# A ReGLU MLP on one core: weight-block sums moved from an engine to accumulating DMAs, with a DMA-turned second half of x, wider output homes and an exit hint

## The chip, the cores and the metric

One core of one Trainium2 chip. The metric is device time in microseconds (us) of one execution; every time below is a median over the runs named. The record sorts executions into fast and slow by their time and the clock granted to TensorE. Engine names in the profile: PE is TensorE's matmul stream, PEld its weight loads, DVE is VectorE, ACT ScalarE, POOL GpSimd, SP SyncE. SPq and POOLq are the issuing sides of those engines.

## The reference

```python
x:  (16, 256, 512)   w1: (512, 4096)   w2: (2048, 512)      # float32
h = x @ w1
gate, value = np.split(h, 2, axis=-1)
h = np.maximum(gate, 0) * value
return (h @ w2).astype(np.float32)
```

## The kernel before

The 4096 rows of x are handled in four *sets* of 1024. Both matmuls are done in float16 by a recursive scheme with seven products of half-size blocks in place of eight. It needs sums of blocks of the weights (T1 to T4) and of the moving operand (S1 to S4):

```python
TURNS = (("T1", "B12", "B11", SUB), ("T2", "B22", "T1", SUB), ("T3", "B22", "B12", SUB), ("T4", "B21", "T2", SUB))
SUMS  = (("S1", "A21", "A22", ADD), ("S2", "S1", "A11", SUB), ("S4", "A12", "S2", SUB), ("S3", "A11", "A21", SUB))
WX = {"P1": ("B11", "A11"), "P2": ("B21", "A12"), "P3": ("B22", "S4"), "P4": ("T4", "A22"),
      "P5": ("T1", "S1"), "P6": ("T2", "S2"), "P7": ("T3", "S3")}
```

The first matmul has 16 *blocks* of hidden columns a set (the first four of the first set are plain products). Its weight sums are the tile `wt`, made chunk by chunk on GpSimd (`w1_ops`). The gated result `g` is the moving side of the second matmul, with its own sums `g_S`. The second matmul's weight sums `v_T` are made once, in the first set, also on GpSimd. In program order, with cuts marked:

```python
if s == 0:
    w1_ops(nc.gpsimd, 4, 2); ...                  # wt of blocks 4-9, loads of w2 between
    for c in range(1, NS):
        cast_x(c)                                 # DRAM to DRAM, f32 to f16, sets 1 to 3, GpSimd's DMA queue
    w1_ops(nc.gpsimd, 10, 2)                      # wt of blocks 10, 11
    w1_ops(nc.gpsimd, 12, 4)                      # wt of blocks 12 to 15
    for m in ("T1", "T2", "T3"):
        w2_op(nc.gpsimd, m)                       # v_T: one 128x2048 tensor_tensor each
for at in ...:                                    # the blocks; products of the last set's second matmul between
    if n == "P1" and s == 0 and jb in (10, 12, 14):
        g_sum(nc.gpsimd, go, "S3", jb - 10, jb - 8)
    ...
if s == 0:
    g_sum(nc.gpsimd, go, "S3", 6, 8)
    w2_op(nc.gpsimd, "T4")
    for m in ("S1", "S2", "S4"):                  # on DVE, two halves each
        for h in (0, NHC // 2):
            g_sum(nc.vector, go, m, h, h + NHC // 2)
```

I call *seam* the stretch from the first product of a set's second matmul to the first block of the next set. In it TensorE has only the second matmul to do, and waits for T and S sums if they are late.

Of the kernel before, what the change touches and what calls it, by code (L numbers as in the profile page):

```python
# [16 lines left out]
P = 128  # L17
TH = 512
PERIOD = 7
NWARM = 7  # L20
NFILL = 4
# [8 lines left out]
@with_exitstack  # L30
def kernel(ctx: ExitStack, tc: tile.TileContext, x, w1, w2, out):






    nc = tc.nc
    x2 = x.flatten_outer_dims()
    out2 = out.flatten_outer_dims()  # L40
    flagpool = ctx.enter_context(tc.tile_pool(name="flagpool", bufs=1))
    flag = flagpool.tile([1, 1], dt.int32, name="flag")
    with ExitStack() as fast:
        unfit = fast_way(fast, tc, x2, w1, w2, out2, flag)
    with tc.If(unfit > 0, preferred_fallthrough_block=False):
        with ExitStack() as general:
            general_way(general, tc, x2, w1, w2, out2)
# [52 lines left out]
def fast_way(ctx, tc, x2, w1, w2, out2, flag):  # L100
# [32 lines left out]
    x16 = {s: dpool.tile([SET, D], F16, name=f"x16_{s}") for s in range(1, NS)}  # L133
# [17 lines left out]
    TURNS = (("T1", "B12", "B11", SUB), ("T2", "B22", "T1", SUB), ("T3", "B22", "B12", SUB), ("T4", "B21", "T2", SUB))  # L151
# [8 lines left out]
    def w2_op(eng, name, n=1):  # L160
        for m, a, b, o in TURNS:
            if m == name:
                for h in range(0, NHC, NHC // n):
                    hs = slice(h, h + NHC // n)
                    eng.tensor_tensor(V[m][:, hs], V[a][:, hs], V[b][:, hs], op=o)

# [3 lines left out]
    ident = {t: wpool.tile([P, P], t, name=f"ident{k}") for k, t in enumerate((F32, F16))}  # L170
# [15 lines left out]
    SUMS = (("S1", "A21", "A22", ADD), ("S2", "S1", "A11", SUB), ("S4", "A12", "S2", SUB), ("S3", "A11", "A21", SUB))  # L186
# [9 lines left out]
    class Block:  # L196
# [25 lines left out]
        def P6(self):  # L222
            self.mm("P6", self.Y, False)
            nc.scalar.activation(self.u2, self.Y, COPY, scale=GS)  # L224
# [9 lines left out]
        def P7(self):  # L234
            self.mm("P7", self.Y, False)
            nc.vector.scalar_tensor_tensor(out=self.c22, in0=self.Y, scalar=GS, in1=self.p5, op0=MULT, op1=ADD)  # L236
# [41 lines left out]
    def mm2_stream(s, go):  # L278
# [14 lines left out]
        def step(name, b):  # L293
# [6 lines left out]
            elif name == "P5":  # L300
                d["W"] = take(psw, "W")
                yield from mm("P5", b, d["W"], True)
                d["pu"] = tmp.tile([P, 2, TH], F32, name="pv", tag="tmp")[:, :, :HALF]
# [5 lines left out]
            elif name == "P6":  # L309
                yield from mm("P6", b, d["Y"], False)  # L310
                nc.scalar.activation(d["pu"][:, 1], d["Y"], COPY, scale=1 / GS)
            elif name == "P3":
                yield from mm("P3", b, d["W"], False)
                nc.vector.scalar_tensor_tensor(out=d["o1"][:, HALF:], in0=d["W"], scalar=1 / GS, in1=d["pu"][:, 1],  # L314
                                               op0=MULT, op1=ADD)
                nc.sync.dma_start(out=out_v[s, 0, b], in_=d["o1"])
            elif name == "P7":
                yield from mm("P7", b, d["Y"], False)
                d["o2"] = tmp.tile([P, DO], F32, name="o", tag="o", bufs=4)
                nc.vector.scalar_tensor_tensor(out=d["o2"][:, HALF:], in0=d["Y"], scalar=1 / GS, in1=d["pu"][:, 0],  # L320
                                               op0=MULT, op1=ADD)
                if last and b == NB - 1:
                    nc.sync.dma_start(out=out_v[s, 1, b, :, HALF:], in_=d["o2"][:, HALF:])
            else:
                yield from mm("P4", b, d["Y"], False)
                if last and b == NB - 1:
                    m = HALF // 2
                    nc.scalar.activation(d["o2"][:, :m], d["Y"][:, :m], COPY, scale=1 / GS)  # L328
                    nc.scalar.dma_start(out=out_v[s, 1, b, :, :m], in_=d["o2"][:, :m])
                    o3 = tmp.tile([P, DO], F32, name="o", tag="o", bufs=4)[:, :m]  # L330
                    nc.vector.tensor_scalar(out=o3, in0=d["Y"][:, m:], scalar1=1 / GS, scalar2=None, op0=MULT)  # L331
                    nc.sync.dma_start(out=out_v[s, 1, b, :, m:HALF], in_=o3)
                else:
                    nc.scalar.activation(d["o2"][:, :HALF], d["Y"], COPY, scale=1 / GS)
                    nc.sync.dma_start(out=out_v[s, 1, b], in_=d["o2"])
# [35 lines left out]
    xh = go["S2"][:, :NB]  # L371
    wl = g[:, NJ - 4:].rearrange("p a t -> p (a t)").bitcast(F32).rearrange("p (e g j) -> p e g j", e=4, g=2)

    def turn_pair(o, b0):
        for b in (b0, b0 + 1):
            ps = psw.tile([P, 4, P], F32, name="W", tag="W")
            for e in range(4):
                nc.tensor.transpose(ps[:, e], xf[:, b, e * P:(e + 1) * P], ident[F32])
# [3 lines left out]
    def turn_half(o, b0, copy):  # L382
        ps = psx.tile([P, 4, 2, P], F16, name="X", tag="X")
        for b in range(2):
            for e in range(4):
                nc.tensor.transpose(ps[:, e, b], xh[:, b0 + b, e * P:(e + 1) * P], ident[F16])
        copy(out=o["A2"][:, :, b0 * P:(b0 + 2) * P], in_=ps.rearrange("p e b t -> p e (b t)"))
# [6 lines left out]

    def look_x(s, i):
        b = i // 2
        t = rows[s, b // 2][:, b % 2] if s else (xf, xh)[b // NB][:, b % NB]
# [6 lines left out]
    fetch_w1(1, 0)  # L404
    make_identity(nc, ident[F32])
    fetch_w1(1, 1)
    nc.gpsimd.dma_start(out=xh[:, :2], in_=x_v[0, :, NB:NB + 2])
    make_identity(nc, ident[F16])
    nc.gpsimd.dma_start(out=xh[:, 2:], in_=x_v[0, :, NB + 2:])
    for c in range(2, len(CHUNKS)):  # L410
# [3 lines left out]
    xo = x_tiles()  # L414
    plain = [Plain(g, jb) for jb in range(NPLAIN)]
# [17 lines left out]
    for p in plain[2:]:  # L433
# [5 lines left out]
        if p is plain[2]:  # L439
            turn_half(xo, 0, nc.vector.tensor_copy)  # L440
    turn_half(xo, 2, nc.scalar.copy)
# [6 lines left out]
    for p in plain:  # L448
        p.open_x()
        p.open_w()  # L450
        if p is plain[0]:
            for q in range(2):
                p.mm(0, xo["A2"], q)
                p.mm(1, xo["A2"], q)
        else:
            p.mm(0, xo["A2"], 0, 2)
            p.mm(1, xo["A2"], 0, 2)
# [11 lines left out]

    def fetch_rows(s, q):  # L470
        rows[s, q] = xpool.tile([P, 2, D], F16, name=f"xn{q % 2}")
        nc.sync.dma_start(out=rows[s, q], in_=x16[s][q * 256:(q + 1) * 256].rearrange("(b p) d -> p b d", p=P))
# [31 lines left out]
    verdict = []  # L504
    BESIDE[NS - 1, 18] = [lambda: verdict.append(nc.values_load(
# [5 lines left out]
    for s in range(NS):  # L511
# [7 lines left out]
        if s == 0:  # L519
# [9 lines left out]
            w1_ops(nc.gpsimd, 10, 2)  # L529
            w1_ops(nc.gpsimd, 12, 4)  # L530
            for m in ("T1", "T2", "T3"):
                w2_op(nc.gpsimd, m)
        for at in range(first * PERIOD, last + PERIOD):
            if at in plan:
# [3 lines left out]
                if n == "P1" and s == 0 and jb in (10, 12, 14):  # L538
                    g_sum(nc.gpsimd, go, "S3", jb - 10, jb - 8)
# [14 lines left out]
        if s == 0:  # L554
            g_sum(nc.gpsimd, go, "S3", 6, 8)
            w2_op(nc.gpsimd, "T4")
            for m in ("S1", "S2", "S4"):
# [6 lines left out]
        if s + 1 < NS:  # L564
            xo = x_tiles()
            for h in range(2):
                for k in range(2):
                    nc.sync.dma_start_transpose(out=xo[f"A{h + 1}{k + 1}"],
                                                in_=x16[s + 1][h * TH:(h + 1) * TH, k * 256:k * 256 + 256])
# [42 lines left out]
```

## Time and profile before

The kernel takes 326.84 us (three runs, 326.08 to 327.3); the profiled execution spans 325.6 us. From the profile's first two parts (busy time and its share of the span; then busy tenths in 40 slices of 8.1 us, and the granted TensorE clock in tenths):

```profile
PE 306.3 (94%) x1868; PEld 183.7 (56%) x1868; DVE 216.9 (67%) x331; ACT 189.0 (58%) x450; POOL 160.3 (49%) x133
...
PE   7999999954999999999999999999999999999892
...
PEclk9999999995999999999999999999999999999998
```

TensorE is the bottleneck, with one visible hole in mid-kernel (the digits 5 and 4), in which the clock also falls to half. The waits of PE name it (line waited at, what released it: total us, times, longest):

```profile
PE Y L285 <- DVE g_S L274: 6.0, 2, 4.4
PE W L285 <- DVE g_S L274: 1.7, 1, 1.7
PE Y L285 <- DVE flag L488: 1.5, 1, 1.5
```

7.7 us are waits for `g_S` sums on DVE, all in the first set's seam; 1.5 us wait for the flag that decides the exit. A further 0.7 us, further down the same list, is for an output tile. Why DVE is late shows in the timelines of the two engines (start us, busy us, engine, line, operation, output<-inputs, count). GpSimd:

```profile
47.52 2.13 POOL L158 TENSOR_TENSOR wt<-wr,wt 128x1024 f16<-128x1024 f16 x1
49.59 4.08 POOL L165 TENSOR_TENSOR v_T<-w_sb 128x2048 f16<-128x2048 f16 x1
53.76 4.07 POOL L165 TENSOR_TENSOR v_T<-w_sb,v_T 128x2048 f16<-128x2048 f16 x1
57.79 4.07 POOL L165 TENSOR_TENSOR v_T<-w_sb 128x2048 f16<-128x2048 f16 x1
61.81 10.32 POOL L274 TENSOR_TENSOR g_S<-g 128x1024 f16<-128x1024 f16 x4
72.10 5.03 POOL L165 TENSOR_TENSOR v_T<-w_sb,v_T 128x2048 f16<-128x2048 f16 x1
```

and DVE:

```profile
65.62 4.53 DVE L274 TENSOR_TENSOR g_S<-g 128x2048 f16<-128x2048 f16 x2
70.08 8.13 DVE L274 TENSOR_TENSOR g_S<-g_S,g 128x2048 f16<-128x2048 f16 x2
78.13 2.35 DVE L274 TENSOR_TENSOR g_S<-g,g_S 128x2048 f16<-128x2048 f16 x2
```

T1 to T3 push S3 to 61.8 and T4 to 72.1, so GpSimd runs beside DVE's sums until 77.1. Each of these DVE lines is a pair of sums: a pair takes 4.5 and 8.1 us beside GpSimd and 2.35 us without it. The Trainium skill, "SBUF — State Buffer", section "Who interferes with whom", says that a DVE instruction with two SBUF inputs contends with a GpSimd instruction that reads SBUF, and that one of the two then waits for the whole of the other; this trace agrees: from the second on, each DVE sum beside GpSimd ends 1.1 us after the GpSimd sum that it met (70.16 after 69.07, 73.22 after 72.14, 78.21 after 77.12).

### The profile page before, as it was taken

To read this page: it belongs to the slowest core of one execution; us is meant where nothing else is said; L and a number is where in the kernel's file an instruction comes from. 1 tells how busy PE (TensorE), PEld (TensorE's weight loads), DVE (VectorE), ACT (ScalarE), POOL (GpSimd) and SP (SyncE) were. 2 spreads that over 40 slices of the span, in tenths; PEclk is the share of its full clock that TensorE was granted. 3 is DMA by queue.
4 is the path that set the end of the run, shared out by engine and by line. 5 is a ranking of instruction groups with operands and counts; after the bars stand their busy time and mean duration, and the time that the engine had idled before them with its cause. 6 is when DMAs were issued, how large, how long until landed. Compare 5 with 4: busy or idle time off the path is not lost. (4 is left out here: it accounts for less than half of the span.)

```text
span 325.6 us, 5158 instructions
## 1 busy us (share of the span) xinstructions
PE 306.3 (94%) x1868; PEld 183.7 (56%) x1868; DVE 216.9 (67%) x331; ACT 189.0 (58%) x450; POOL 160.3 (49%) x133
## 2 busy tenths in 40 slices
PE   7999999954999999999999999999999999999892
PEld 3754444543884444458884444448884444448681
DVE  1377888898736888885525888886525888886210
ACT  3347666532756766755757666665757666663120
POOL 8499999994001334994001344995001344995000
PEclk9999999995999999999999999999999999999998
DMA  7999995260321100026311100018411100000222
GB/s 242 209 203 207 237 204 123 64 131 0 129 81 50 35 32 0 0 44 153 132 64 66 32 30 4 0 31 140 155 67 64 32 31 4 0 2 0 99 85 84
DMA packets 30542, 26.60 MB, mean 82 GB/s; under 512 B 13776, under 2 KB 25936, under 8 KB 30416
## 3 DMA queue, kind: packets, MB, share of 16 engines
q0 software_dynamic: 8080, 9.44, 16.8%
q1 hardware_dynamic: 21232, 15.67, 16.3%
q10 hardware_dynamic: 1200, 1.11, 1.1%
q8 instruction: 16, 0.26, 0.3%
q14 instruction: 14, 0.11, 0.1%
HBM read 24.12 MB, written 11.53 MB: 109 GB/s over the span
## 5 line engine op out<-in xcount | busy, mean ns | idle before, releaser
L274 POOL TENSOR_TENSOR g_S<-g 128x512 f16<-128x512 f16 (+1 forms) x46 | 58.8, 1281 | 127.0 <-DVE g L240 125.1
L203 PEld LDWEIGHTS <-wt 128*128 128x128 f16 x480 | 46.8, 97 | 56.2 <-issue 2.5
L203 PE MATMUL X<-x_A,wr 128*128 128x512 f16 x240 | 71.3, 378 | 0.2 <-ACT Y L210 0.2
L203 PE MATMUL Y<-x_S,wt 128*128 128x512 f16 x240 | 71.4, 379 | 0.0
L230 DVE SCALAR_TENSOR_TENSOR cc<-W,pu 128x512 f32<-128x512 f32 x60 | 41.5, 692 | 35.1 <-ACT pu L224 35.1
L285 PEld LDWEIGHTS <-g_S 128*128 128x128 f16 x512 | 50.5, 99 | 15.0 <-DVE g_S L274 8.5
L203 PEld LDWEIGHTS <-wr 128*128 128x128 f16 x360 | 35.0, 97 | 41.2 <-issue 0.5
L210 ACT COPY Y<-X 128x512 f32<-128x512 f32 x60 | 34.2, 570 | 38.6 <-PE X L203 19.8
L224 ACT ACTIVATE pu<-Y 128x512 f32<-128x512 f32 x60 | 35.8, 597 | 14.4 <-PE Y L203 14.4
L285 PEld LDWEIGHTS <-g 128*128 128x128 f16 x384 | 37.5, 98 | 10.9 <-issue 2.7
L231 DVE SCALAR_TENSOR_TENSOR g<-X,cc 128x512 f16<-128x512 f32 x60 | 41.5, 691 | 2.3
L240 DVE SCALAR_TENSOR_TENSOR g<-Y,cc 128x512 f16<-128x512 f32 x60 | 40.9, 681 | 2.8 <-PE Y L203 2.8
L236 DVE SCALAR_TENSOR_TENSOR cc<-Y,pu 128x512 f32<-128x512 f32 x60 | 40.9, 681 | 0.1
L285 PE MATMUL Y<-v_T,g_S 128*128 128x256 f16 x256 | 32.0, 279 | 6.0 <-DVE g_S L274 6.0
L217 ACT ACTIVATE pu<-W 128x512 f32<-128x512 f32 x60 | 36.2, 603 | 0.0
L203 PE MATMUL W<-x_S,wt 128*128 128x512 f16 x120 | 35.7, 379 | 0.0
L203 PE MATMUL W<-x_S,wr 128*128 128x512 f16 x120 | 35.7, 379 | 0.0
L203 PE MATMUL Y<-x_A,wt 128*128 128x512 f16 x120 | 35.5, 377 | 0.0
L285 PE MATMUL X<-w_sb,g 128*128 128x256 f16 x256 | 31.2, 273 | 0.0
L314 DVE SCALAR_TENSOR_TENSOR o<-W,pv 128x256 f32<-128x256 f32 x16 | 6.8, 425 | 34.3 <-PE W L285 25.0
L274 POOL TENSOR_TENSOR g_S<-g,g_S 128x512 f16<-128x512 f16 x18 | 21.8, 1213 | 1.4
L274 POOL TENSOR_TENSOR g_S<-g_S,g 128x512 f16<-128x512 f16 x18 | 20.8, 1155 | 1.4
(69 smaller groups left out, 315.3 us busy)
## 6 DMA issues: line engine op xcount, KB each, us to landing
out_dram<-o SPq DMA_DIRECT2D x31, 256.0 KB, 2.0
x<-in_x_dram POOLq DMA_DIRECT2D x3, 1024.0 KB, 15.1
xn<-x SPq DMA_DIRECT2D x12, 256.0 KB, 2.9
wr<-in_w_dram POOLq DMA_DIRECT2D x4, 512.0 KB, 14.4
w_sb<-in_w_dram POOLq DMA_DIRECT2D x4, 512.0 KB, 11.3
wr<-in_w_dram POOLq DMA_DIRECT2D x6, 256.0 KB, 10.3
g<-in_w_dram ACTq DMA_DIRECT2D x2, 512.0 KB, 7.1
g_S<-in_x_dram SPq DMA_DIRECT2D x2, 512.0 KB, 5.8
```

Source lines behind the costliest of these rows:

```text
L203: nc.tensor.matmul(ps, W(wn, self.jb)[:, b], self.xo[xn][:, b, :], start=fresh and b == 0, stop=b == 1, skip_group_check=True)
L210: nc.scalar.copy(out=self.Y, in_=self.X)
L217: nc.scalar.activation(self.p5, self.W, COPY, scale=GS)
L224: nc.scalar.activation(self.u2, self.Y, COPY, scale=GS)
L230: nc.vector.scalar_tensor_tensor(out=self.c12, in0=self.W, scalar=GS, in1=self.u2, op0=MULT, op1=ADD)
L231: nc.vector.scalar_tensor_tensor(out=self.g[:, self.jb, :TH], in0=self.X, scalar=0.0, in1=self.c12, op0=MAX, op1=MULT)
L236: nc.vector.scalar_tensor_tensor(out=self.c22, in0=self.Y, scalar=GS, in1=self.p5, op0=MULT, op1=ADD)
L240: nc.vector.scalar_tensor_tensor(out=self.g[:, self.jb, TH:], in0=self.Y, scalar=0.0, in1=self.c22, op0=MAX, op1=MULT)
L274: eng.tensor_tensor(go[n][:, h0:h1], go[i0][:, h0:h1], go[i1][:, h0:h1], op=op)
L285: nc.tensor.matmul(ps, go[gn][:, k, b * P:(b + 1) * P], V[vn][:, k, :], start=fresh and k == 0, stop=k == NHC - 1, skip_group_check=True)
L314: nc.vector.scalar_tensor_tensor(out=d["o1"][:, HALF:], in0=d["W"], scalar=1 / GS, in1=d["pu"][:, 1], op0=MULT, op1=ADD)
```

## The change

Four things at once.

1. All weight sums become additions (the signs move into S1, S4 and the scales of P6 and P7), so that T1 to T4 of w2 can be made by a plain copy and an accumulating DMA, off GpSimd's arithmetic. The time so freed on GpSimd takes S3 earlier and three quarters of S1 from DVE.
2. The second half of the first set's x is cast in DRAM and turned by DMA transposes, in place of a load and 16 transposes on TensorE.
3. The second output tile of a block lives in the other half of its `pv` tile, not in the shared pool `o`.
4. The exit branch gets a hint; the last output goes out in one piece a side.

The core of the diff, cuts marked by "...":

```diff
-    TURNS = (("T1", "B12", "B11", SUB), ("T2", "B22", "T1", SUB), ("T3", "B22", "B12", SUB), ("T4", "B21", "T2", SUB))
+    TURNS = (("T1", "B12", "B11", ADD), ("T2", "B22", "T1", ADD), ("T3", "B22", "B12", ADD), ("T4", "B21", "T2", ADD))
-    SUMS = (("S1", "A21", "A22", ADD), ("S2", "S1", "A11", SUB), ("S4", "A12", "S2", SUB), ("S3", "A11", "A21", SUB))
+    SUMS = (("S1", "A21", "A22", SUB), ("S2", "S1", "A11", SUB), ("S4", "A12", "S2", ADD), ("S3", "A11", "A21", SUB))
...
-                d["pu"] = tmp.tile([P, 2, TH], F32, name="pv", tag="tmp")[:, :, :HALF]
+                t = tmp.tile([P, 2, TH], F32, name="pv", tag="tmp")
+                d["pu"], d["o2"] = t[:, 0].rearrange("p (a n) -> p a n", a=2), t[:, 1]
...
-    nc.gpsimd.dma_start(out=xh[:, :2], in_=x_v[0, :, NB:NB + 2])
-    nc.gpsimd.dma_start(out=xh[:, 2:], in_=x_v[0, :, NB + 2:])
+    nc.gpsimd.dma_start(out=x16[0][TH:], in_=x2[TH:SET, :])
...
+    turn_by_dma(0, xo, 1)          # in place of turn_half: TensorE transposes of xh
...
+    BESIDE[NS - 1, 20] = [lambda: tc.mark_branch_hint_location("general")]
...
             w1_ops(nc.gpsimd, 10, 2)
+            nc.sync.dma_start(out=V["T1"], in_=V["B11"])
+            nc.sync.dma_start(out=V["T3"], in_=V["B12"])
+            nc.gpsimd.dma_start(out=V["T1"], in_=V["B12"], accum_op=ADD)
+            nc.gpsimd.dma_start(out=V["T3"], in_=V["B22"], accum_op=ADD)
+            nc.sync.dma_start(out=V["T2"], in_=V["T1"])
             w1_ops(nc.gpsimd, 12, 4)
-            for m in ("T1", "T2", "T3"):
-                w2_op(nc.gpsimd, m)
+            nc.gpsimd.dma_start(out=V["T2"], in_=V["B22"], accum_op=ADD)
+            nc.sync.dma_start(out=V["T4"], in_=V["T2"])
...
-                if n == "P1" and s == 0 and jb in (10, 12, 14):
-                    g_sum(nc.gpsimd, go, "S3", jb - 10, jb - 8)
+                if n == "P1" and s == 0 and jb in (11, 12, 13, 14):
+                    g_sum(nc.gpsimd, go, "S3", 2 * jb - 22, 2 * jb - 20)
+                    if jb == 12:
+                        nc.gpsimd.dma_start(out=V["T4"], in_=V["B21"], accum_op=ADD)
...
-            g_sum(nc.gpsimd, go, "S3", 6, 8)
-            w2_op(nc.gpsimd, "T4")
-            for m in ("S1", "S2", "S4"):
+            for h in (0, 2, 4):
+                g_sum(nc.gpsimd, go, "S1", h, h + 2)
+            g_sum(nc.vector, go, "S1", 6, 8)
+            for m in ("S2", "S4"):
```

The order on GpSimd: the accumulates into T1 and T3 stand before `w1_ops(12, 4)`, and each must wait for its copy, which SP issues.

More of the change, by code (lines that the diff above doesn't have):

```diff
@@ L19 @@
 PERIOD = 7
-NWARM = 7
-NFILL = 4
+NWARM = 8
+NFILL = 2
 NPLAIN = 4
@@ L44 @@
         unfit = fast_way(fast, tc, x2, w1, w2, out2, flag)
-    with tc.If(unfit > 0, preferred_fallthrough_block=False):
+    with tc.If(unfit > 0, label="general"):
         with ExitStack() as general:
@@ L132, in fast_way @@
     v_t = {n: wpool.tile([P, NHC, HALF], F16, name=f"v_{n}") for n in ("T1", "T2", "T3", "T4")}
-    x16 = {s: dpool.tile([SET, D], F16, name=f"x16_{s}") for s in range(1, NS)}
+    x16 = {s: dpool.tile([SET, D], F16, name=f"x16_{s}") for s in range(NS)}
     NX = 2 * 2 * NB * NS
@@ L158, in w1_ops @@
         turned(lambda m, a, b, o: eng.tensor_tensor(W(m, jb, n), W(a, jb, n), W(b, jb, n), op=o))
-    def w2_op(eng, name, n=1):
-        for m, a, b, o in TURNS:
-            if m == name:
-                for h in range(0, NHC, NHC // n):
-                    hs = slice(h, h + NHC // n)
-                    eng.tensor_tensor(V[m][:, hs], V[a][:, hs], V[b][:, hs], op=o)
     warm = tmp.tile([P, 2, TH], F32, name="warm", tag="tmp")
@@ L169, in fast_way @@
     nc.vector.memset(warm[:, 0], 0.0)
-    ident = {t: wpool.tile([P, P], t, name=f"ident{k}") for k, t in enumerate((F32, F16))}
+    ident = wpool.tile([P, P], F32, name="ident")
     def idle(n):
@@ L223, in P6 @@
             self.mm("P6", self.Y, False)
-            nc.scalar.activation(self.u2, self.Y, COPY, scale=GS)
+            nc.scalar.activation(self.u2, self.Y, COPY, scale=-GS)
         def P3(self):
@@ L235, in P7 @@
             self.mm("P7", self.Y, False)
-            nc.vector.scalar_tensor_tensor(out=self.c22, in0=self.Y, scalar=GS, in1=self.p5, op0=MULT, op1=ADD)
+            nc.vector.scalar_tensor_tensor(out=self.c22, in0=self.Y, scalar=-GS, in1=self.p5, op0=MULT, op1=ADD)
         def P4(self):
@@ L310, in step @@
                 yield from mm("P6", b, d["Y"], False)
-                nc.scalar.activation(d["pu"][:, 1], d["Y"], COPY, scale=1 / GS)
+                nc.scalar.activation(d["pu"][:, 1], d["Y"], COPY, scale=-1 / GS)
             elif name == "P3":
@@ L318, in step @@
                 yield from mm("P7", b, d["Y"], False)
-                d["o2"] = tmp.tile([P, DO], F32, name="o", tag="o", bufs=4)
-                nc.vector.scalar_tensor_tensor(out=d["o2"][:, HALF:], in0=d["Y"], scalar=1 / GS, in1=d["pu"][:, 0],
+                nc.vector.scalar_tensor_tensor(out=d["o2"][:, HALF:], in0=d["Y"], scalar=-1 / GS, in1=d["pu"][:, 0],
                                                op0=MULT, op1=ADD)
@@ L325, in step @@
                 yield from mm("P4", b, d["Y"], False)
+                nc.scalar.activation(d["o2"][:, :HALF], d["Y"], COPY, scale=1 / GS)
                 if last and b == NB - 1:
-                    m = HALF // 2
-                    nc.scalar.activation(d["o2"][:, :m], d["Y"][:, :m], COPY, scale=1 / GS)
-                    nc.scalar.dma_start(out=out_v[s, 1, b, :, :m], in_=d["o2"][:, :m])
-                    o3 = tmp.tile([P, DO], F32, name="o", tag="o", bufs=4)[:, :m]
-                    nc.vector.tensor_scalar(out=o3, in0=d["Y"][:, m:], scalar1=1 / GS, scalar2=None, op0=MULT)
-                    nc.sync.dma_start(out=out_v[s, 1, b, :, m:HALF], in_=o3)
+                    nc.scalar.dma_start(out=out_v[s, 1, b, :, :HALF], in_=d["o2"][:, :HALF])
                 else:
-                    nc.scalar.activation(d["o2"][:, :HALF], d["Y"], COPY, scale=1 / GS)
                     nc.sync.dma_start(out=out_v[s, 1, b], in_=d["o2"])
@@ L370, in fast_way @@
     xf = go["S1"].rearrange("p a t -> p (a t)").bitcast(F32).rearrange("p (b d) -> p b d", b=NB)
-    xh = go["S2"][:, :NB]
     wl = g[:, NJ - 4:].rearrange("p a t -> p (a t)").bitcast(F32).rearrange("p (e g j) -> p e g j", e=4, g=2)
@@ L377, in turn_pair, with turn_by_dma @@
             for e in range(4):
-                nc.tensor.transpose(ps[:, e], xf[:, b, e * P:(e + 1) * P], ident[F32])
+                nc.tensor.transpose(ps[:, e], xf[:, b, e * P:(e + 1) * P], ident)
             copy = nc.scalar.copy if b % 2 else nc.vector.tensor_copy
             copy(out=o["A1"][:, :, b * P:(b + 1) * P], in_=ps)
-    def turn_half(o, b0, copy):
-        ps = psx.tile([P, 4, 2, P], F16, name="X", tag="X")
-        for b in range(2):
-            for e in range(4):
-                nc.tensor.transpose(ps[:, e, b], xh[:, b0 + b, e * P:(e + 1) * P], ident[F16])
-        copy(out=o["A2"][:, :, b0 * P:(b0 + 2) * P], in_=ps.rearrange("p e b t -> p e (b t)"))
+    def turn_by_dma(s, o, h):
+        for k in range(2):
+            nc.sync.dma_start_transpose(out=o[f"A{h + 1}{k + 1}"], in_=x16[s][h * TH:(h + 1) * TH, k * 256:k * 256 + 256])
     def cast_w(g_):
@@ L393, in fast_way, with fetch_rows @@
     rows = {}
+    def fetch_rows(s, q):
+        rows[s, q] = xpool.tile([P, 2, D], F16, name=f"xn{q % 2}")
+        nc.sync.dma_start(out=rows[s, q], in_=x16[s][q * 256:(q + 1) * 256].rearrange("(b p) d -> p b d", p=P))
     def look_x(s, i):
         b = i // 2
-        t = rows[s, b // 2][:, b % 2] if s else (xf, xh)[b // NB][:, b % NB]
+        t = rows[s, b // 2][:, b % 2] if (s, b // 2) in rows else xf[:, b]
         look(t[:, i % 2 * 256:i % 2 * 256 + 256], 4 * NB * s + i, 256)
@@ L403, in fast_way @@
         nc.scalar.dma_start(out=wl[:, :, g_], in_=w1_v[:, :, g_, :2 * P])
-    fetch_w1(1, 0)
-    make_identity(nc, ident[F32])
-    fetch_w1(1, 1)
-    nc.gpsimd.dma_start(out=xh[:, :2], in_=x_v[0, :, NB:NB + 2])
-    make_identity(nc, ident[F16])
-    nc.gpsimd.dma_start(out=xh[:, 2:], in_=x_v[0, :, NB + 2:])
-    for c in range(2, len(CHUNKS)):
+    make_identity(nc, ident)
+    nc.gpsimd.dma_start(out=x16[0][TH:], in_=x2[TH:SET, :])
+    for c in range(1, len(CHUNKS)):
         for g_ in range(2):
@@ L414, in fast_way @@
     xo = x_tiles()
+    turn_by_dma(0, xo, 1)
+    for q in (2, 3):
+        fetch_rows(0, q)
     plain = [Plain(g, jb) for jb in range(NPLAIN)]
@@ L438, in fast_way @@
         p.close(0)
-        if p is plain[2]:
-            turn_half(xo, 0, nc.vector.tensor_copy)
-    turn_half(xo, 2, nc.scalar.copy)
     sums = list(SUMS)
@@ L450, in fast_way @@
         p.open_w()
-        if p is plain[0]:
-            for q in range(2):
-                p.mm(0, xo["A2"], q)
-                p.mm(1, xo["A2"], q)
-        else:
-            p.mm(0, xo["A2"], 0, 2)
-            p.mm(1, xo["A2"], 0, 2)
+        p.mm(0, xo["A2"], 0, 2)
+        p.mm(1, xo["A2"], 0, 2)
         x_sum(xo)
@@ L468, in look_w2 @@
         look(w2_sb[:, 2 * i:2 * i + 2].rearrange("p h n -> p (h n)"), NW + i, 1024)
-    def fetch_rows(s, q):
-        rows[s, q] = xpool.tile([P, 2, D], F16, name=f"xn{q % 2}")
-        nc.sync.dma_start(out=rows[s, q], in_=x16[s][q * 256:(q + 1) * 256].rearrange("(b p) d -> p b d", p=P))
     def judge():
@@ L566, in fast_way @@
             for h in range(2):
-                for k in range(2):
-                    nc.sync.dma_start_transpose(out=xo[f"A{h + 1}{k + 1}"],
-                                                in_=x16[s + 1][h * TH:(h + 1) * TH, k * 256:k * 256 + 256])
+                turn_by_dma(s + 1, xo, h)
             for q in range(2):
```

## The prediction

> **Bound now.** TensorE: 306 of 325.6 us busy (page, part 1). Its waits (waits view, PE): 7.7 us on the DVE block sums g_S, all between 68 and 78 us; 1.5 us on flag; 0.7 us on o. The first set's seam (first product of the second matmul to the next set's first block) takes 61.77 to 95.92 = 34.15 us; the same work takes 218.50 to 243.13 = 24.63 us in the third set (timeline). Excess 9.5 us: the waits, plus TensorE's clock, which the 4.4 us wait drops to 0.5 from 74.5 to 81.4 us. The Trainium skill, "TensorE: Matmul & The Clock Gate", says an idle window of about 3.4 us does that; this trace agrees.
>
> Behind it: GpSimd makes T1 to T3 of w2 (4.07 us each), then S3 until 72 and T4 until 77. DVE starts S1, S2, S4 at 65.6; beside GpSimd its 128x2048 sums take 3 to 5 us, not 1.2, so S4 ends at 80.5.
>
> **Removed, added, moved.**
> - T1 to T4 leave GpSimd (17.3 us). Instead: four copies on SP, four accumulating DMAs issued by GpSimd (about 1 us each, an estimate from a load's 0.75).
> - S3 moves ahead, three quarters of S1 move to GpSimd; DVE keeps S2 and S4, 1.2 us per half when alone. If GpSimd reaches S3 by 55 us, S1 is ready near 67 (wanted 66.8), S2 by 69, S4 by 71.5: the seam loses 1 to 2 us, not 9.5, and the clock stays up.
> - Risk: the accumulates stand in GpSimd's DMA queue behind the three x casts, which land at 45.8, 50.6 and 55.4 us (DMA view). T2's copy needs T1's accumulate, and GpSimd waits for that copy before S3. Then S3 starts near 58 to 60, S1 ends near 74, and only 2 to 4 us of the 9.5 return. Worse, SP's copies share engines over 90% busy until 53 us; the skill ("DMA: Bandwidth & Descriptors", Queues, rings and completion order) says each engine alternates between queues by packet. Behind cast packets of 1.2 to 2.4 us, T3's copy could hold GpSimd before the w1 sums of block 12, wanted at 50 us; then TensorE stalls there. This trace has no such overlap.
> - Start: 16 transposes on TensorE (1.3 us) go; the second x half waits for its cast (first in queue, near 11 us) and two DMA transposes (3.5 us each alone, slower beside loads), wanted at 17.4. Net -1 to +2 us; I take 0.
> - o in the pv tile: frees DVE of the 2.3 us wait for an output DMA at 307 that holds the flag: -1.5 to -2.2 us. The block reusing that buffer at each seam may wait up to 0.3 us.
> - Exit: TensorE's final branch takes 4.1 us (319.3 to 323.4), but the last output lands at 323.1 to 323.3 anyway: about -0.2.
>
> **Prediction.** 318.5 us; 8 in 10 within 311 to 330. Faster by over 2%: 0.55; within 2%: 0.35; slower: 0.10.
>
> **What would show it.** Right: TensorE's waits on g_S under 3 us, no 0.5 clock in mid-kernel, seam under 28 us, no wait on flag, GpSimd's S3 before 60. Wrong: GpSimd idle on a v_T DMA between 42 and 65 us, TensorE waiting on wt near 50 to 56 or on x_A near 18 to 22, a seam still over 31 us.
>
> **Would make it wrong:** T copies or accumulates landing after 60 us, or the second x half after 19.

## The result

The kernel after takes 345.5 us (median of four runs, 344.94 to 345.71) against 327.07 us for before in the same rounds (326.08 to 328.6). The ratio is 1.056, 95% interval 1.051 to 1.060: slower. The outputs are right. Ratios here and below are the mean time of one kernel's fast runs over that of the other's of the same rounds, so not quite the ratio of the medians quoted. The profiled execution spans 343.2 us.

The page of after, the same lines:

```profile
PE 308.5 (90%) x1843; PEld 182.0 (53%) x1843; DVE 217.8 (63%) x328; ACT 188.1 (55%) x449; POOL 152.6 (44%) x133
...
PE   6589993099469999999999999999999999999993
...
PEclk9789999579969999999999999999999999999999
```

There are now three holes: in slices 0 to 2 (the start), in slices 6 and 7 (51 to 69 us), and in slices 10 and 11 (the seam), each with a lower clock. Cutting both spans at the same points of the program, read from the matmul records, gives the account (us):

| stretch | before | after | difference |
|---|---|---|---|
| start to first product with a `wt` (block 4) | 26.18 | 30.84 | +4.66 |
| blocks 4 to 15 of the first set | 35.59 | 51.94 | +16.35 |
| first seam | 34.15 | 34.63 | +0.48 |
| from there to the last matmul | 223.20 | 220.55 | -2.65 |
| tail after the last matmul | 6.50 | 5.20 | -1.30 |
| span | 325.6 | 343.2 | +17.5 |

So what was to gain 8 us, the seam, gained nothing; a stretch that had next to no waits now loses 16 us; and only the small parts (output homes, tail) gave what they promised, or a little more. The waits of PE in after:

```profile
PE W L196 <- POOL wt L158: 13.8, 1, 13.8
PE W L278 <- POOL g_S L267: 7.8, 3, 4.7
```

The first is the big hole: TensorE waits 13.8 us for the w1 sums of block 12. What GpSimd was doing instead is in its own timeline; a bracket gives the idle time before an instruction and what ended it:

```profile
63.23 1.65 POOL L508 DMA_DIRECT2D v_T<-w_sb  x1 [20.43 <-DMA v_T<-w_sb]
64.73 1.75 POOL L509 DMA_DIRECT2D v_T<-w_sb  x1
65.67 2.96 POOL L158 TENSOR_TENSOR wt<-wr 128x1024 f16<-128x1024 f16 x1
...
76.73 4.85 POOL L267 TENSOR_TENSOR g_S<-g 128x1024 f16<-128x1024 f16 x2
85.85 1.56 POOL L522 DMA_DIRECT2D v_T<-w_sb  x1 [4.28 <-DMA v_T<-v_T]
86.80 11.03 POOL L267 TENSOR_TENSOR g_S<-g 128x1024 f16<-128x1024 f16 x5
```

GpSimd is idle for 20.4 us at the accumulate into T1, which waits for T1's copy. The `wt` sums behind it start at 65.67, where before had made all of them by 49.6. SP had issued the copies long ago:

```profile
40.73 0.72 SPq L506 DMA_DIRECT2D v_T<-w_sb  x1
41.49 0.68 SPq L507 DMA_DIRECT2D v_T<-w_sb  x1
```

and the DMA view (operation, engine, count, size, median time to landing) says where the time is:

```profile
v_T<-w_sb POOLq DMA_DIRECT2D x4, 512.0 KB, 8.3
...
v_T<-w_sb SPq DMA_DIRECT2D x2, 512.0 KB, 22.3
```

A 512 KB copy inside the core takes 22 us, while an accumulate (the line of POOLq) takes 8.3. The chain of work that ended last (start us, us, what) runs through T1's copy, then GpSimd's `wt` sums, into TensorE at half clock (two matmuls in 0.85 us, and 0.43 from 73.8 on):

```profile
40.73 21.87 DMA v_T<-w_sb
...
69.72 0.85 PE Y L196 x2
...
74.27 0.43 PE W L196 x2
```

The Trainium skill, "TensorE: Matmul & The Clock Gate", Part 1, says that an idle window of about 3.4 us halves the clock; the trace agrees: in this 13.8 us wait the granted clock falls to half at 59.9 us, 5 us after the last matmul, and stays there until 73.6 us, about 2.5 us of loss on top of the wait (the stretch's 16.35 us less the wait). The fall in before's seam is a less clear case than the prediction made it: the clock record falls at 74.5 us, only 0.6 us into the 4.4 us wait, and the 3.4 us before it hold 1.2 us of matmuls, so shorter waits counted too.

In the seam, DVE's part of S1 is one 128x1024 sum:

```profile
86.77 11.62 DVE L267 TENSOR_TENSOR g_S<-g 128x1024 f16<-128x1024 f16 x1
98.31 2.35 DVE L267 TENSOR_TENSOR g_S<-g_S,g 128x2048 f16<-128x2048 f16 x2
```

It takes 11.62 us and ends at 98.39, 0.6 us after GpSimd's row of five sums (86.80 to 97.83), where even 128x2048 takes 1.2 us undisturbed.

### The profile page after: what moved, and what is told of

The parts are those of the page before. It is cut to its first block, busy times and chain, and to the rows that moved or that the text cites. A ratio compares the mean times of both kernels' runs of the same rounds, so it can differ in the third digit from the quotient of the medians.

```text
span 343.2 us, 5085 instructions
## 1 busy us (share of the span) xinstructions
PE 308.5 (90%) x1843; PEld 182.0 (53%) x1843; DVE 217.8 (63%) x328; ACT 188.1 (55%) x449; POOL 152.6 (44%) x133
## 4 chain that ended last, share of the span: by engine, by line
PE 75%; DMA 15%; POOL 7%; issue 1%; DVE 0%; ACT 0%; POOLq 0%; SPq 0%
PE Y L196 20%; PE W L196 13%; PE X L196 13%; PE Y L278 12%; PE W L278 9%; PE X L278 7%; DMA v_T<-w_sb 6%; DMA w_sb<-in_w_dram 5%; DMA wr<-in_w_dram 4%; POOL g_S L267 3%; POOL wt L158 2%; POOL wr L344 1%; POOL v_T L509 1%; POOL v_T L508 0%; POOL w_sb L347 0%
## 5 line engine op out<-in xcount | busy, mean ns | idle before, releaser
L267 POOL TENSOR_TENSOR g_S<-g 128x512 f16<-128x512 f16 (+1 forms) x49 | 64.4, 1382 | 126.8 <-DVE g L233 124.8
L196 PE MATMUL Y<-x_S,wt 128*128 128x512 f16 x240 | 72.3, 383 | 0.0
L203 ACT COPY Y<-X 128x512 f32<-128x512 f32 x60 | 34.2, 570 | 39.3 <-PE X L196 20.5
L196 PE MATMUL W<-x_S,wt 128*128 128x512 f16 x120 | 36.1, 383 | 13.8 <-POOL wt L158 13.8
L217 ACT ACTIVATE pu<-Y 128x512 f32<-128x512 f32 x60 | 35.9, 598 | 15.3 <-PE Y L196 15.3
L196 PE MATMUL Y<-x_A,wt 128*128 128x512 f16 x120 | 35.9, 380 | 0.0
L278 PE MATMUL Y<-v_T,g_S 128*128 128x256 f16 x256 | 30.7, 273 | 0.0
L278 PE MATMUL W<-v_T,g_S 128*128 128x256 f16 x128 | 17.9, 288 | 7.8 <-POOL g_S L267 7.8
L184 ACT ACTIVATE sq<-xn 128x256 f16<-128x256 f16 x56 | 23.2, 415 | 0.0
```

The source lines that it names most:

```text
L184: nc.scalar.activation(sq, t, SQUARE, scale=(P / of) ** 0.5, accum_out=st[:, at:at + 1])
L196: nc.tensor.matmul(ps, W(wn, self.jb)[:, b], self.xo[xn][:, b, :], start=fresh and b == 0, stop=b == 1, skip_group_check=True)
L203: nc.scalar.copy(out=self.Y, in_=self.X)
L217: nc.scalar.activation(self.u2, self.Y, COPY, scale=-GS)
L267: eng.tensor_tensor(go[n][:, h0:h1], go[i0][:, h0:h1], go[i1][:, h0:h1], op=op)
L278: nc.tensor.matmul(ps, go[gn][:, k, b * P:(b + 1) * P], V[vn][:, k, :], start=fresh and k == 0, stop=k == NHC - 1, skip_group_check=True)
```

## The theories

Why did the copy take 22 us? The trace's DMA packet records, counted by queue in stretches of 2 us (packets from all 16 engines; q0 is GpSimd's queue with the x casts, q1 is SP's with the copies). Each 1 MB cast ends with a 4-byte record on every engine, which counts here as a packet; so a median of 4 B or 16386 B stands for a mixture of 32768 and 4:

```
after          q0 packets, median size      q1 packets, size
46 to 48 us    15   32768 B (2431 ns each)     15   512 B
48 to 50       31   32768 B                    31   512 B
50 to 52       16   32768 B                    16   512 B
52 to 54       12   32768 B                    12   512 B
54 to 56       22   16386 B                    22   512 B
56 to 58       15   32768 B                    16   512 B
58 to 60       15       4 B                   624   512 B
60 to 62        2       4 B                  1202   512 B
```

While both queues have work, the counts are equal: each engine takes one packet of the one queue, then one of the other. The Trainium skill, "DMA: Bandwidth & Descriptors", section "Queues, rings and completion order", says that each engine goes round its queues by packet; the trace agrees, one for one. A cast packet takes 2.43 us, and the two copies together have 2048 small packets, 128 on each engine, of which some 120 in all (seven or eight an engine) go before 58 us. The casts have only six 32 KB packets on each engine (96 records). When they end, on most engines near 59 us and on the last at 60.5, the rest is done, by 63.7.

- **Theory 1 (packets).** Turn by turn, a 512-byte packet waits for one 32 KB packet. Smaller cast packets, or casts out of the way, free the copies and with them GpSimd and block 12.
- **Rival 1 (bytes).** The engines are full with the casts' bytes anyway; whatever the packets, the copies land when the casts have. With casts of six packets an engine against copies of 64, theory 1 gives nearly the same landing; only a change of the packets can part the two.
- **Rival 2 (the sums by DMA themselves).** The accumulates and their chain (copy, accumulate, copy, accumulate) are slow, and would be late without the casts too.
- **For the seam**: either S3 and S1 are late only because GpSimd was held, or the new division of S1 between GpSimd and DVE costs by itself.
- **For the start**: the DRAM cast of x and the DMA transposes share the engines with the first loads; or the start is unlucky and the new start is no worse.

## Experiments

Twelve kernels ran. Each row of this table is one, timed against before on the same chip (after itself was not timed again there; its ratio from the first rounds is 1.056, 1.051 to 1.060); all were correct.

| run | us | ratio to before (95%) |
|---|---|---|
| after, casts of sets 1 to 3 in 1 KB packets | 342.55 | 1.045 (1.042 to 1.048) |
| after, all casts in 1 KB packets | 343.25 | 1.047 (1.043 to 1.050) |
| after, casts issued later | 347.16 | 1.060 (1.056 to 1.063) |
| after, with the start of before | 340.36 | 1.039 (1.036 to 1.041) |
| after, S1 wholly on DVE | 340.97 | 1.041 (1.035 to 1.048) |
| before, signs only | 327.42 | 0.999 (0.995 to 1.004) |
| before, signs and T1 to T4 by DMA | 338.70 | 1.034 (1.029 to 1.039) |
| before, output homes only | 325.12 | 0.992 (0.989 to 0.995) |
| before, exit hint only | 327.22 | 0.997 (0.994 to 1.001) |
| only T2, T3, T4 by DMA | 323.06 | 0.987 (0.982 to 0.992) |
| only T3, T4 by DMA | 316.82 | 0.969 (0.965 to 0.973) |
| the same, S1 three quarters on GpSimd | 323.74 | 0.990 (0.985 to 0.995) |

### Smaller cast packets

The casts of sets 1 to 3 keep their bytes, but name them row by row:

```diff
-        nc.gpsimd.dma_start(out=x16[s], in_=x2[s * SET:(s + 1) * SET, :])
+        nc.gpsimd.dma_start(out=x16[s].rearrange("(b p) d -> p b d", p=P),
+                            in_=x2[s * SET:(s + 1) * SET, :].rearrange("(b p) d -> p b d", p=P))
```

> The kernel after, with the casts of the sets 1 to 3 written so that a packet is one row of 1 KB, not 32 KB: same bytes, same queue, same order. Theory P (an engine gives each queue one packet in turn, so behind cast packets of 2.4 us a 512-byte copy packet advances once per cast packet): T1's copy lands by about 50 us, not 63; GpSimd's wait for it falls from 20.4 to under 8 us, TensorE's wait on the w1 sums of block 12 from 13.8 to under 2, no half clock near 60 to 73 us, the kernel takes 329 to 334 us. Rival Q (the engines are full, bytes decide): nothing changes by over 3 us, about 345. Rival R (copies of 512-byte pieces and accumulates are slow in themselves): likewise about 345. The start and the seam stay as they are in all three.

Measured 342.55 us, 3 us better than after, and short of what was expected. The packet records confirm the turn-taking: with 1 KB packets of 96 ns the counts are again equal, but now some 280 each in 2 us (275 and 277 from 46 to 48 us). GpSimd gets past T1's accumulate at 53.4 us instead of 63.2. Yet it stays held, because T3's accumulate comes next and T3's copy stands behind T1's in SP's queue. GpSimd's waits in this run:

```profile
POOL v_T L509 <- DMA v_T<-w_sb: 9.8, 1, 9.8
POOL v_T L510 <- DMA v_T<-w_sb: 6.4, 1, 6.4
```

Together 16.2 us in place of 20.4. TensorE's wait on `wt` falls only from 13.8 to 11.2 us:

```profile
PE W L196 <- POOL wt L158: 11.2, 1, 11.2
```

Rival 1 falls in its strict form: T1's copy lands at 52.8 us and the copies' last packets end at 60.4, while the casts' last end at 65.1. This is the run that parts theory 1 from rival 1, by its trace and not by its time. But theory 1's expectation was a miscount of mine. With 128 copy packets an engine, each waiting for a cast packet of 96 ns and taking 40 ns itself, the two copies need some 17 us even so (an estimate from these durations; the records show 15, from 45 to 60 us). Small packets in equal turns do not free a copy that has as many packets as this one.

### All casts smaller

The same edit for the cast of the second x half (16 KB rows cut to 1 KB) in addition.

> As a_small_123, and the cast of the second half of the first x set in packets of 1 KB too. Theory P: the loads of x and w beside it are no longer held for two long packets, so TensorE's two gaps of 2.45 and 2.14 us before 14 us shrink to under 2 us in sum, the half clock from 12 to 19 us goes, and the first block of seven products starts at 28.5 to 30 us, not 30.4 (less than the gaps give, since the cast now lands later and the transposed half with it): 0.5 to 3 us below a_small_123. Rival Q: same start as in a_small_123.

Measured 343.25 us: no better. At the start the x load's gap on TensorE goes (its wait falls from 2.2 to 0.4 us), but the gap at the w load stays (2.5 us in the waits view, 1.9 in after), and the cast itself, now one in many turns, lands later (11.7 us), the transposes behind it run until about 26.7, and PE waits 6.2 us on `x_A`. The first `wt` product comes at 36.3 us instead of 30.8. It pays some of that back: reaching block 12 later, TensorE waits only 4.3 us there. Expectation missed; the start has no cheap cure by packet size.

### Casts after the accumulates

```diff
-            for c in range(1, NS):
-                cast_x(c)
             w1_ops(nc.gpsimd, 10, 2)
             ... copies and accumulates of T1 and T3 ...
+            for c in range(1, NS):
+                cast_x(c)
```

> The kernel after, with the casts of sets 1 to 3 (still 32 KB packets) issued after the accumulates into T1 and T3. Theory P and rival Q: both copies land by about 49 us, GpSimd waits under 7 us, block 12 no longer waits (under 2 us), 329 to 337 us. Theory P adds: T2's copy, 8 packets of 4 KB on each engine, now stands beside the casts and takes over 8 us from issue to landing, not the 4 to 5 us of the kernel after, so the seam keeps its loss. Rival R: the accumulates still hold T2's chain, and GpSimd still waits over 15 us for the copies.

Measured 347.16 us, where 329 to 337 was expected, and no better than after (1.060 against 1.056, with intervals that overlap). Yet the part under test did what theory 1 and rival 1 both say: with no cast beside them both copies finish within 5 us of their first packet (43.9 to 48.6 us), and block 12 loses 1.1 us instead of 13.8. Against this landing rival 2 does not hold. But the next copy, T2 from T1, is now the one beside the casts. GpSimd's waits in this run, then PE's:

```profile
POOL v_T L512 <- DMA v_T<-v_T: 15.9, 1, 15.9
POOL v_T L506 <- DMA v_T<-w_sb: 7.4, 1, 7.4
```

```profile
PE W L278 <- POOL g_S L267: 24.1, 3, 21.1
```

T2's copy, with 4 KB packets and thus only eight on each engine, was issued at 55.4 us, had its first packet at 60.6 (why so late, no run explains), took turns with the casts' packets (12 and 12 packets from 66 to 68 us, 23 and 25 from 68 to 70), and held GpSimd until 77.3. Its last packet ended at 76.6 us, the casts' last 32 KB packet at 76.4. So this run does not part theory 1 from rival 1: on each engine six cast packets of 2.43 us or more stood against the copy's eight, and both were through together. What it shows is that the casts hold the copy: one of the same size and packets landed 2.9 us after its issue in the best kernel below, with no cast beside it. S3 and S1 stand behind it, and the seam grows to 51.3 us. Moving the casts only moves the collision.

### The start of before, in after

The load `xh`, TensorE's transposes of it, the fetch order and the numbers of warm-up matmuls are put back; all else is after.

> The kernel after with the start of the kernel before (second x half cast into SBUF and turned by TensorE, 7 and 4 warm matmuls); the rest as after. Theory: the start's 4.6 us come back (first block at 25.5 to 26.5 us), and since w2 lands 3 to 4 us earlier, more of T1's copy is through before the casts; GpSimd is still held at the accumulates into T1 and T3 until about 58 to 60 us. 335 to 341 us. A rival by which the loss in the middle comes from the late start (everything 5 us late) would bring over 10 us back.

Measured 340.36 us, as expected: 5.1 us better than after. The first `wt` product comes at 26.23 us, as in before. GpSimd still waits 16.5 us at T1's accumulate and TensorE 13.1 us for `wt`, so start and middle are separate losses.

In after's own trace the start shows three holes. The cast's packets (16 of 2431 ns between 6 and 8 us) stand beside the first loads, and TensorE has gaps of 2.45 us at the x load (8.5 to 11.0) and 2.1 us at the w load (11.8 to 13.9), from the start of one matmul to that of the next; as waits (the second is for the copy of x on DVE, which stands behind the cast of w there):

```profile
PE W L365 <- DMA g_S<-in_x_dram: 2.5, 2, 2.2
PE W L251 <- DVE x_A L367: 1.9, 1, 1.9
```

The clock falls to half from 12.1 to 19.0 us; and the two transposes, issued at 9.94, have 256-byte packets in equal turns with the w1 loads (496 and 503 packets from 18 to 20 us), so that they last from 14.1 to 23.4 us.

### Parts alone, on before

Signs only (the two tables and the scales of P6 and P7):

> The kernel before with the signs of the change alone: all block sums of w added, the signs moved into the x sums and into four scales. Both theories: no cost and no gain, within 0.3% (1 us), since a sum takes as long as a difference (1.15 us per 128x512 on GpSimd either way).

Measured 0.999 of before: nothing, as it should be, since the same instructions run with another operator.

Signs, and T1 to T4 by copies and accumulating DMAs in the order of after; start, S division, homes and exit of before:

> The kernel before with the signs and with T1 to T4 by copies and accumulating DMAs, at the places the change gives them; start, block sums of g, o homes and exit as before. Theory P: the copies' 512-byte packets stand against the casts' 32 KB packets, T1's copy lands near 57 to 59 us, GpSimd waits 15 to 18 us there, TensorE waits 11 to 14 us on the w1 sums of block 12, its clock halves once more; 337 to 343 us, so this part alone is worse than the whole change, less its start. A rival by which the new division of the block sums of g (S1 on GpSimd) is what costs: under 330 us.

Measured 338.7 us, +3.4%, about 11 us. The largest part of after's loss is here alone: GpSimd waits 16.7 us, TensorE waits 13.3 us on `wt`. Its seam, with the old division of S, takes 30.2 us, shorter than before's 34.2: the sums gained half of what the prediction hoped for, but behind a stall that costs more.

The output homes, with the last output in one piece a side as in after:

> The kernel before with o2 kept in the pv tile, and the last output written by one DMA. Expected from the trace: DVE's wait for an output DMA at 307 us (2.3 us) and TensorE's wait for the flag (1.5 us) go, also its 0.7 us on o at 158 us: 1.5 to 2.5 us faster. If DVE's wait at 307 was not what held TensorE: no change.

Measured 0.992 (about -2.7 us), a little more than predicted. The waits on `flag` and on `o` are gone from PE's list.

The hint alone:

> The kernel before with the hint and the other layout of the final branch alone. As predicted blind: 0 to 0.4 us faster, as the last output lands at 323.1 to 323.3 us and TensorE's branch ends at 323.4. The rival, from the trace after, where 5.2 us and not 6.5 lie between the last matmul and the end: 0.8 to 1.4 us faster.

Measured 0.997 with an interval that holds 1. In the profile the branch on PE now starts 1.2 us before the last matmul ends (318.82 against 320.04) and the tail shrinks from 6.5 to 5.2 us. The time says at most that; it is not resolved.

### The division of S1

In after, S1 goes back to DVE; GpSimd keeps S3 only:

```diff
-            for h in (0, 2, 4):
-                g_sum(nc.gpsimd, go, "S1", h, h + 2)
-            g_sum(nc.vector, go, "S1", 6, 8)
-            for m in ("S2", "S4"):
+            for m in ("S1", "S2", "S4"):
                 for h in (0, NHC // 2):
                     g_sum(nc.vector, go, m, h, h + NHC // 2)
```

> The kernel after, but S1 wholly on DVE as before; all else as after. So far the parts tried alone do not add up: signs, T by DMA, o homes and hint with the old division of the block sums give about 335 by adding their differences, the same with the new division (a_start_before) measures 340.4. Theory: with GpSimd late, its three S1 pieces end the chain (S1 at 98 us in the kernel after), and DVE's own piece is blocked behind them; with S1 on DVE the seam falls from 34.6 to 30 to 31 us, 340 to 342 us in all, and all else stays. If the new division is innocent: no change, 345.

Measured 340.97 us, 4.5 us better than after, as expected. The seam falls from 34.6 to 30.8 us. So the new division costs by itself, when GpSimd comes late. The reverse test, the new division in the best kernel (below), follows there.

### Only the sums that nobody waits for

If a DMA-made sum is bad only where GpSimd must wait for a slow copy, then the gain should be had by choosing sums whose copies have time. Kernel one: signs, homes and hint; T1 on GpSimd as before; T2, T3 and T4 by DMA, accumulates placed among the blocks; S division as in before.

> The kernel before with signs, o homes and hint, and with T2, T3 and T4 (not T1) by copy and accumulate, placed so that no wait of GpSimd or TensorE stands behind the casts: T3's copy is started when w2 has landed, T1 is a GpSimd sum after the w1 sums of block 12, then half of S3, and only then (casts landed at 55 us) the accumulates into T3 and T2; T4's accumulate last. Theory P: no wait on the w1 sums of block 12, GpSimd ends its S3 by 67 us and not 72, DVE's block sums run nearly alone, the seam takes 26 to 30 us and not 34, 315 to 321 us. If copies and accumulates were slow in themselves or the half-finished T4 held the seam: 325 us or more.

Measured 323.06 us, faster than before but short of what was expected. The stall at block 12 is gone. But T4 needs T2's accumulate and then a copy, GpSimd issues the last accumulate only at 72.8 us after waiting 6.2 us for that copy, and TensorE waits for T4:

```profile
PE Y L285 <- DMA v_T<-w_sb: 5.3, 1, 5.3
```

In the profiled execution the start was also 1.6 us longer than in before, with the same code there. Here rival 2 holds in part: after the casts, the accumulate into T2 was issued at 59.1 us and that into T4, one copy later, only at 72.8. In after, too, the chain ran from the accumulate into T1 at 63.2 us to that into T4 at 85.9 with no cast beside it, each link issued within a microsecond of the landing of the one before.

Kernel two makes T1 and T2 on GpSimd; only T3 and T4, the ends of the chain, go by DMA:

```diff
             w1_ops(nc.gpsimd, 10, 2)
+            nc.sync.dma_start(out=V["T3"], in_=V["B12"])
             w1_ops(nc.gpsimd, 12, 4)
-            for m in ("T1", "T2", "T3"):
+            for m in ("T1", "T2"):
                 w2_op(nc.gpsimd, m)
+            nc.sync.dma_start(out=V["T4"], in_=V["T2"])
...
-                if n == "P1" and s == 0 and jb in (10, 12, 14):
-                    g_sum(nc.gpsimd, go, "S3", jb - 10, jb - 8)
+                if n == "P1" and s == 0 and jb in (11, 12, 13, 14):
+                    g_sum(nc.gpsimd, go, "S3", 2 * jb - 22, 2 * jb - 20)
+                    if jb == 12:
+                        nc.gpsimd.dma_start(out=V["T3"], in_=V["B22"], accum_op=ADD)
+                    if jb == 14:
+                        nc.gpsimd.dma_start(out=V["T4"], in_=V["B21"], accum_op=ADD)
...
-            g_sum(nc.gpsimd, go, "S3", 6, 8)
-            w2_op(nc.gpsimd, "T4")
```

> The same with T1 and T2 on GpSimd and only T3 and T4 by DMA: one accumulate less in the chain but 4 us more work on GpSimd, S3 ends near 70 us. Theory P: seam 28 to 31 us, 317 to 323 us, so between best_T234 and b_homes (325).

Measured 316.82 us (316.4 to 317.08), ratio 0.969: it beats both kernels. That is just under the range expected, and the order was expected the other way round, this kernel slower than kernel one. The line of the clock no longer has a hole in mid-kernel, PE's waits on `g_S` fall from 7.7 us to 2.2 (the line shown, and one of 0.3), and DVE's S2 runs at full speed, and so does S4 (2.35 us from 72.23; the clock's line; PE's waits; DVE's timeline):

```profile
PEclk9999999999999999999999999999999999999998
```

```profile
PE W L285 <- DVE g_S L274: 1.9, 3, 1.1
```

```profile
65.48 4.56 DVE L274 TENSOR_TENSOR g_S<-g 128x2048 f16<-128x2048 f16 x2
69.96 2.35 DVE L274 TENSOR_TENSOR g_S<-g_S,g 128x2048 f16<-128x2048 f16 x2
```

The seam takes 27.4 us in place of 34.2. T3's copy is no faster here: it is issued at 35.9 us and lands 21.2 us later, again in turns with the casts. Nobody needs it before 61.9 us, where its accumulate is issued without a wait.

The last kernel gives this one the division of S1 of after:

> best_T34 with the division of S1 that the change makes (three quarters on GpSimd, one on DVE). There GpSimd ends S3 at 67.8 us and its accumulate at 69.3, so three S1 pieces end near 76 us, and S2 waits for them: seam 32 to 35 us and not 27.4, 321 to 325 us. If the division helped whenever GpSimd is not held by DMAs: 316 or less.

Measured 323.74 us, 6.9 us worse than without, as expected. DVE's quarter of S1 and GpSimd's three quarters (timelines of the two engines):

```profile
65.73 10.56 DVE L274 TENSOR_TENSOR g_S<-g 128x1024 f16<-128x1024 f16 x1
```

```profile
68.18 7.55 POOL L274 TENSOR_TENSOR g_S<-g 128x1024 f16<-128x1024 f16 x3
```

The three GpSimd pieces are its part of S1. The DVE sum ends at 76.29, half a microsecond after the last of them. With S1 on DVE it had both its halves by 70.0. What speaks against this division is GpSimd's time: 2.1 us or more for a 128x1024 piece. That DVE's own piece does not get in between GpSimd's adds only about half a microsecond. In after with small cast packets it did run alone, before GpSimd's row (DVE, then GpSimd):

```profile
82.20 0.69 DVE L267 TENSOR_TENSOR g_S<-g 128x1024 f16<-128x1024 f16 x1
```

```profile
84.11 11.04 POOL L267 TENSOR_TENSOR g_S<-g 128x1024 f16<-128x1024 f16 x5
```

GpSimd's row of S3 and S1 took as long as in after (11.03 us), S1 was complete only at its end, 95.1, and the seam took 36.5 us. It went the same way with all casts small and with the casts late.

## Why the prediction was wrong

The prediction was 318.5 us, a gain, and the result 345.5, a loss.

- **The step that failed** is the one that begins "If GpSimd reaches S3 by 55 us": S3 began at 76.7 us, and the seam cost 34.6 us where I had put about 26. GpSimd was not free to reach S3: it stood 20.4 us at the accumulate into T1, for T1's copy. The seam term, some -8 us in my sum, measured +0.5. Behind it lies a condition on a DMA's landing, and I took the landing for granted.
- **The case that came true was written down, as "Worse", and given too little weight.** I named T3's copy (it was T1's, ahead of it, that held most) behind cast packets of 1.2 to 2.4 us (the records of 32 KB show 2.43 throughout), GpSimd held, TensorE stalled at block 12. The size needed only a multiplication I did not do. Two copies of 512 KB in 512-byte packets are 128 packets on each of 16 engines; at one cast packet of 2.4 us a turn, they cannot land before the casts do, near 55 us by before's own trace. With the start late too, the casts ended at 59 to 60.5 and T1's copy landed at 62.6. The term that I left at no cost measured +16.35 us.
- **"Net -1 to +2 us; I take 0"** for the start measured +4.7 us in the profile and 5.1 us in the run with before's start. I had reckoned the transposes at 3.5 us each; the pair lasted 9.3 us beside the loads, and the cast also delayed the first x and w loads, which I had not thought of.
- **The new division of S1** I counted as help, from DVE's and GpSimd's single times. The runs say it costs 4.5 us in after and 6.9 in the best kernel, since S1 is complete only when GpSimd's three pieces are, at 2.1 us or more each and behind S3; I had reckoned with a GpSimd that comes early.
- **Right**: the output homes (-1.5 to -2.2 predicted, -2.7 measured, the last output in one piece included), what the wait list would show if I was wrong (but for the wait on `x_A`, 0.9 us near 23 us and not between 18 and 22), and that a seam without DVE's and GpSimd's clash is worth about 8 us: the best kernel's seam gained 6.7. The exit's -0.2 is not contradicted: the timed effect of the hint, -0.3% with an interval to 0, is unresolved.

The parts, each measured alone, about make the whole: T sums by DMA +11.1 us (ratio 1.034 of 327), start +5.1, division of S1 +4.5, homes -2.7, hint -0.9, signs 0: +17.1, against +17.5 in the profile and +18.2 by the ratio. They were measured on two different bases and in different rounds, so their interplay is not excluded, and some of the close agreement is luck.

What stays open. No run put `w1_ops(12, 4)` ahead of T1's accumulate in after and changed nothing else; block 12 would then lose its stall by the logic of the waits, but S3 would still stand behind the copies. No run gave the copies of T1 and T3 fewer, larger packets. And why DVE's sum gets no turn between GpSimd's in the seam, when in before its 128x2048 sums did alternate with GpSimd's (DVE's second half of S1 ran beside two GpSimd sums that ended at 69.07 and 72.14, and was itself done at 70.16), no run explains. In each trace where it was kept out, an accumulating DMA had been issued on GpSimd just before, and the records of GpSimd's sums overlap by about 0.65 us or more; that is an observation, not a cause.

## What to carry to other kernels

Work moved from an engine to a DMA costs nothing only if nobody must wait for the landing: count its packets per DMA engine, multiply by the packet time of the queue that is busy beside it (up to the time at which that queue runs empty), and look at what stands behind the waiting instruction in its engine's program order. In the best kernel here the DMAs had the ends of the chain of sums, not the head, and the copies started long before they were needed. And before splitting one sum over two engines that block each other, compare it with the faster of them doing all of it alone.

## What the Trainium skill lacked or had wrong

- "DMA: Bandwidth & Descriptors", section "Queues, rings and completion order": it says that an engine alternates between queues by packet, of some 9 to 17 descriptors, typically. The alternation is confirmed (15 and 15, 31 and 31, 16 and 16 packet records in 2 us), but one for one in records of 512 B against 32 KB, whatever their size (whether a record is one such packet, no run shows); the page does not draw the consequence that a copy in small packets beside a cast in large ones is held until the cast ends (512 KB took 22 us, and 5 us for two of them from first packet to last with the casts away).
- The same page, section "SWDGE vs HWDGE vs iDMA", puts a packet at preferably 4096 bytes or less. The DRAM-to-DRAM cast of whole rows on GpSimd's queue ran in records of 32768 bytes, 2431 ns each; a row-by-row view of the same bytes gave 1024 bytes and 96 ns.
- No page has the speed of an accumulating DMA inside the core: 512 KB landed 8.3 us after issue (median of four), with packets of 512 bytes, most of 64 to 86 ns; by first and last packet, T1's and T3's together ran at 127 GB/s, T2's at 133 and T4's, beside the transposes and loads of the next set, at 71.
- "DMA: Bandwidth & Descriptors", section "Latency and other measured facts", gives DMA transposes 261 to 400 GB/s. The two at the start had 256-byte packets and took 9.3 us beside loads in equal turns; before's later transposes landed in 3.6 us (median of twelve). No page says what a transpose costs beside other queues.
- "SBUF — State Buffer", section "Who interferes with whom": it says that issue order decides who blocks. In after DVE's sum has a record from 86.77 and GpSimd's row one from 86.80, yet DVE's ended only at 98.39, after all five of GpSimd's (97.83). The page does not say that the one that lost can lose again to each following instruction.
